# Computing the first memory attention's keys and values at the start of the kernel instead of under the recurrence

## The chip, the cores and the metric

The kernel runs on one core of a Trainium2 chip. Its time is device microseconds for one execution; three runs gave 3854.62, 3855.39 and 3858.6 us, and the median, 3855.39 us, is the time before. A core has five engines with a queue each: TensorE (PE, matrix products), VectorE (DVE), ScalarE (ACT), GpSimd (POOL) and SyncE (SP, which here issues most transfers). Sixteen DMA engines carry all transfers between DRAM and on-chip memory.

## The reference

Two stacks run one after the other on 256 tokens of width 2048, in float32. The first is two layers of attention with pooling and Fourier branches; each layer is modulated by a shift, a scale and a gate that come from a condition vector. The second has an even layer (sparse attention and an RWKV recurrence, joined by one output projection), an odd layer (a state space mixer), and after each a cross attention to 256 memory tokens and an MLP. The two pieces that the change touches are the memory's keys and values and the projection:

```python
shift, scale, gate = jnp.split(jax.nn.silu(c) @ ada_w[l] + ada_b[l], 3, axis=-1)   # first stack
h = rmsnorm(x, norm_g[l]) * (1.0 + scale[:, None]) + shift[:, None]

mix = jnp.concatenate([y_a, y_b], axis=-1) @ even_w_out[i]                         # second stack, even layer
x = x + mix
kv = (rms_norm(mem, norm_mem[layer]) @ wkv).reshape(bsz, mem.shape[1], 2, X_HEADS, X_HEAD_DIM)
```

The memory does not depend on anything that the kernel computes, so its keys and values can be had at any time. `y_a @ even_w_out[:1024]`, half of the output projection, is ready to run once the sparse attention is done; the recurrence gives `y_b`.

## The kernel before, in words

Every large product follows one pattern. `raw` (L309 to L315) issues one transfer of 512 KB of weights from SP into a tile `wraw`; `split` (L303) has ACT cast it into a high part `wh` (L308) and DVE subtract that to a low part `wl` (L309); PE multiplies high by high, high by low and low by high into PSUM tiles `acc` (L344 to L352, or L392 and L393 in `dense_p`). In the first stack there are three buffers of each of `wraw`, `wh` and `wl`; PSUM has four `acc` and four `sm`.

At the start (`layer1`, L780 on, with `l = 0`) the kernel loads the residual `xc` by eight transfers on ACT's queue, squares it for its norm, and streams 64 tiles of the condition's weights `ada_w`, 512 KB each, through three kinds of buffer in turn (`STAGS`: `wraw`, `wl`, `ada_raw`); each feeds two short matmuls (L543). From the twentieth tile in program order on, a step of the first product with `w_in` (`pool_gen`) follows every eighth tile. The tokens are modulated in four groups (`scaled`), as soon as their columns of the condition are there.

A queue of background generators `bg` fills in elsewhere: `tick` advances its first entry, at a lower priority. The instructions of all engines are then put in order by a scheduler that weighs priorities and estimated times, so that their order is not the one in which the code is written.

In the even layer (`even`, L1487) the recurrence goes: preparation of head group 0 (`rwkv_prep`, `rwkv_mats`), with the second group's keys and values (`rkv_stream`) behind it; preparation of group 1; the inverse of 64x64 triangular blocks (`rwkv_inv`), which is 31 pairs of DVE operations on a tile that went through DRAM (`MD`), with its result back through DRAM (`XD`, `YD`); the scan over chunks (`rwkv_seq`); the finish (`rwkv_fin`). The background under the preparation of group 1 is the half output projection (`dense_p(WO, 0, 8, ...)`, sixteen steps of sixteen matmuls, each pair of steps ending in four adds to the residual, L526). Under the inverse and the scan it is `memkv(0, ...)` (L1596), sixteen steps: eight times, 256 KB of `memT` scaled and split (L489, L490) and multiplied by two tiles of `xattn_wkv`. Its norm's statistic is `mem_stat` (L963), a background of the first layer's end that reads `memT` a first time through `wraw`. The keys and values are written to `kv` after the finish (`mkv[0]()`).

Of the kernel before, what the change touches and what calls it, by code (L numbers as in the profile page):

```python
# [10 lines left out]
F32 = mybir.dt.float32  # L11
# [202 lines left out]
class Prog:  # L214
# [575 lines left out]
    def layer1(self, l, xc, adac, st, st_out):  # L790
# [8 lines left out]
        with ExitStack() as es:  # L799
# [10 lines left out]
            with self.pool(f"pl{l}") as pp, self.pool(f"nrm{l}") as p:  # L810
# [16 lines left out]
                if not last:  # L827
# [7 lines left out]
                    adas = [self.ada(0, part, cb, adac, p) for cb in range(4) for part in range(2)]  # L835
                    for i in range(8 * 8):
                        b, j = divmod(i, 8)
                        next(adas[b])
                        if b and j == SJ:
                            next(adas[b - 1], None)  # L840
                            if b % 2 == 0:
                                scaled(b // 2 - 1)
# [9 lines left out]
                    self.bg.append(self.mem_stat())  # L852
# [110 lines left out]
    def mem_stat(self):  # L963
# [4 lines left out]
        for k in range(0, KT, 2):  # L968
            w = self.wp.tile([128, KB, 512], F32, name="wraw", bufs=self.wraw)[:, :, :T]
            nc.sync.dma_start(w, mT[:, k:k + 2])  # L970
            self.stat_add(st, w)
            yield
# [3 lines left out]
        nc.scalar.copy(self.mrb, self.bcast(self.mrc, 2)[:, :T])  # L976
        yield
# [507 lines left out]
    def even(self, xc, st, kv, st_out):  # L1485
# [4 lines left out]
        with ExitStack() as es:  # L1490
# [32 lines left out]
            with self.pool("rw0") as rp:  # L1523
# [11 lines left out]
                self.bg.append(self.dense_p(WO, 0, 8, 0, D, Xa, self.add_evac(x)))  # L1535
                with self.pool("rw1") as rp1:
# [5 lines left out]
                    with self.pool("rwb") as p:  # L1542
                        mkv = []
                        self.rwkv_room(s1, p)
                        self.rwkv_mats(s1, BKt)
                        self.flush()
                        room = yp.tile([128, 8, 2, T], F32R, name="mem0", tag="ya")
                        self.bg.append(self.memkv(0, kv[0], kv[1], p, room, mkv))
# [12 lines left out]
                        mkv[0]()  # L1561
# [34 lines left out]
    def memkv(self, l, kT, vN, p, room=None, end=None):  # L1596
# [5 lines left out]
        for k0 in range(0, KT, KB):  # L1602
            m = p.tile([128, KB, T], F32, name="mm", bufs=2)
            i = KB * (k0 // KB % 2)
            hl = p.tile([128, KB, 2, T], F32R, name="mhl", bufs=2) if room is None else room[:, i:i + KB]
# [16 lines left out]
        def evac():  # L1622
            for i in range(2):
                nc.vector.tensor_tensor(kT[:, 2 * i:2 * i + 2], ka[i], self.mrb.unsqueeze(1).to_broadcast([128, 2, T]), op=ALU.mult)
                nc.scalar.mul(vN[:, i], va[i], self.mrc[:, i:i + 1])
        if end is None:
            evac()
        else:
            end.append(evac)
# [408 lines left out]
    def body(self):  # L2038
# [13 lines left out]
        self.wraw, self.wbuf = WR, WB  # L2052
        with self.pool("w1") as self.wp, self.pool("b1") as p:
            st = self.first(xc, p)
# [121 lines left out]
```

## Time and profile before

| what | before |
|---|---|
| median of three runs | 3855.39 us |
| profiled execution | 3850.04 us |
| its span | 3848.3 us |
| PE busy / DVE busy / ACT busy | 95% / 70% / 44% of the span |
| mean granted clock of PE | 0.975 of full |
| DMA, whole span | 182 GB/s, 700.74 MB |

The profiled execution's time is 1.7 us more than its span, and all times of the trace are counted from the span's start. A view "by stretch" gives, for each stretch, the time that each engine was busy, then the granted clock of PE, the busy share of the DMA engines and the rate. A view "by line" groups instructions by code line and says what the engine waited for before them. PE's matmuls overlap each other in the trace, so the mean duration of one is longer than the time it adds.

### The profile page before, as it was taken

What the parts mean: (1) busy time and instruction counts of PE and PEld (TensorE: products, weight loads), DVE (VectorE), ACT (ScalarE), POOL (GpSimd) and SP (SyncE); (2) the same over time, 40 slices, a digit from 0 to 9 for tenths busy, and PEclk for the clock granted to TensorE, in tenths of its full rate; (3) what the DMA queues carried; (4) which work ended last, traced back from release to release, by engine and by line L of the source; (5) the groups of instructions that cost most, each with busy time, mean ns of one, the idle gap of its engine ahead of it and who ended that gap; (6) DMA issues with size and microseconds to landing.
All of it is one profiled execution on the core that took longest, in us unless ns stands there. A gap on an engine that the chain in (4) does not pass through costs nothing.

```text
span 3848.3 us, 54892 instructions
## 1 busy us (share of the span) xinstructions
PE 3654.7 (95%) x21008; PEld 3029.0 (79%) x21008; DVE 2694.8 (70%) x4732; ACT 1680.5 (44%) x2524; POOL 102.1 (3%) x138
## 2 busy tenths in 40 slices
PE   6999999989999999899999999999879999999997
PEld 2677777777678889777888888887778788888886
DVE  3568777765776878767987778786666676656565
ACT  3313233262564566425544444444325454445353
POOL 0010000001000001000000000000000000000000
PEclk8999999999999999889999999999989999999999
DMA  9745544555655544524666666668985556666664
GB/s 343 244 145 176 158 149 156 175 170 174 215 152 158 142 137 140 164 67 145 188 214 197 208 200 208 198 211 247 223 197 181 165 154 191 187 191 187 190 186 148
DMA packets 609335, 700.74 MB, mean 182 GB/s; under 512 B 52208, under 2 KB 493680, under 8 KB 605744
## 3 DMA queue, kind: packets, MB, share of 16 engines
q1 hardware_dynamic: 576304, 662.39, 57.1%
q10 hardware_dynamic: 31488, 30.64, 2.4%
q0 software_dynamic: 1280, 4.20, 0.4%
q8 instruction: 165, 2.70, 0.3%
q14 instruction: 98, 0.80, 0.1%
HBM read 672.63 MB, written 24.51 MB: 181 GB/s over the span
## 4 chain that ended last, share of the span: by engine, by line
PE 82%; DMA 9%; DVE 6%; ACT 2%; issue 1%; SPq 0%; ACTq 0%; POOL 0%; DVEq 0%; POOLq 0%
PE acc L392 33%; PE acc L393 17%; PE acc L344 4%; PE acc L345 4%; PE acc L346 4%; PE acc L350 3%; PE acc L352 3%; PE acc L351 3%; DMA wraw<-ada_w 2%; DVE wl L309 2%; PE sm L623 1%; ACT wh L308 1%; PE sm L600 1%; DMA wraw<-w_in 1%; DMA tts<-KD 1%
## 5 line engine op out<-in xcount | busy, mean ns | idle before, releaser
L308 ACT CAST wh<-wraw 128x1024 fp32r<-128x1024 f32 x994 | 1037.7, 1045 | 1486.3 <-PE acc L392 734.1
L309 DVE TENSOR_TENSOR wl<-wraw,wh 128x1024 fp32r<-128x1024 f32 x994 | 1208.5, 1217 | 643.8 <-ACT wh L308 639.6
L392 PE MATMUL acc<-hl,wh 128*128 128x512 f32 x3008 | 1060.4, 400 | 21.9 <-DVE hl L490 15.1
L393 PE MATMUL acc<-hl,wl 128*128 128x256 f32 x3008 | 827.3, 284 | 4.3 <-DVE wl L309 4.3
L392 PE MATMUL acc<-hid,wh 128*128 128x512 f32 x2048 | 709.9, 394 | 1.4 <-DVE xc L526 1.0
L392 PEld LDWEIGHTS acc<-hl,wh 128*128 128x128 f32 x3008 | 559.3, 190 | 150.4 <-DVE hl L490 11.6
L393 PEld LDWEIGHTS acc<-hl,wl 128*128 128x128 f32 x3008 | 567.9, 190 | 23.4 <-DVE wl L309 8.1
L393 PE MATMUL acc<-hid,wl 128*128 128x256 f32 x2048 | 559.8, 280 | 0.0
L392 PEld LDWEIGHTS acc<-hid,wh 128*128 128x128 f32 x2048 | 378.3, 188 | 85.6 <-issue 1.8
L393 PEld LDWEIGHTS acc<-hid,wl 128*128 128x128 f32 x2048 | 380.9, 188 | 9.0 <-issue 3.4
L571 DVE SCALAR_TENSOR_TENSOR ada_a<-wraw,sc,ada_a 128x512 f32<-128x512 f32 x360 | 253.5, 749 | 19.6 <-DMA wraw<-ada_w 18.7
L344 PE MATMUL acc<-hl,wh 128*128 128x512 f32 (+2 forms) x688 | 256.0, 376 | 7.7 <-ACT wh L308 3.8
L345 PE MATMUL acc<-hl,wh 128*128 128x512 f32 (+2 forms) x688 | 252.9, 369 | 0.0
L346 PE MATMUL acc<-hl,wl 128*128 128x512 f32 (+2 forms) x688 | 247.1, 369 | 0.0
L350 PE MATMUL acc<-wh,hl 128*128 128x512 f32 (+1 forms) x504 | 200.1, 402 | 4.0 <-ACT wh L308 2.5
L351 PE MATMUL acc<-wh,hl 128*128 128x512 f32 (+1 forms) x504 | 199.7, 396 | 0.0
L352 PE MATMUL acc<-wl,hl 128*128 128x512 f32 (+1 forms) x504 | 189.2, 395 | 4.4 <-DVE wl L309 4.4
L526 DVE TENSOR_TENSOR xc<-acc,xc 128x256 f32<-128x256 f32 x384 | 141.8, 419 | 36.7 <-PE acc L393 36.1
L344 PEld LDWEIGHTS acc<-hl,wh 128*128 128x128 f32 (+1 forms) x688 | 130.2, 190 | 37.3 <-issue 6.6
L345 PEld LDWEIGHTS acc<-hl,wh 128*128 128x128 f32 (+1 forms) x688 | 130.0, 189 | 25.2 <-issue 5.9
L346 PEld LDWEIGHTS acc<-hl,wl 128*128 128x128 f32 (+1 forms) x688 | 129.1, 189 | 23.9 <-issue 3.2
L406 ACT COPY joined<-acc 128x256 f32<-128x256 f32 x188 | 69.5, 371 | 133.1 <-PE acc L393 133.0
(588 smaller groups left out, 4950.0 us busy)
## 6 DMA issues: line engine op xcount, KB each, us to landing
wraw<-ffn_up SPq DMA_DIRECT2D x256, 512.0 KB, 3.8
wraw<-ffn_down SPq DMA_DIRECT2D x256, 512.0 KB, 3.7
wraw<-ada_w SPq DMA_DIRECT2D x192, 512.0 KB, 4.5
wraw<-w_in SPq DMA_DIRECT2D x144, 512.0 KB, 4.4
wraw<-w_out SPq DMA_DIRECT2D x64, 512.0 KB, 4.5
wraw<-even_w_in SPq DMA_DIRECT2D x54, 512.0 KB, 3.7
wraw<-even_w_out SPq DMA_DIRECT2D x32, 512.0 KB, 3.6
wraw<-xattn_wkv SPq DMA_DIRECT2D x32, 512.0 KB, 4.7
```

The costliest lines, as they stand in the source:

```text
L308: nc.scalar.copy(hi, src)
L309: self.held(nc.vector.tensor_tensor(lo, src, hi.bitcast(F32), op=ALU.subtract))
L344: nc.tensor.matmul(A, h, xh, start=(start and first), stop=False)
L345: nc.tensor.matmul(A, h, xl, start=False, stop=False)
L346: nc.tensor.matmul(A, lo, xh, start=False, stop=(stop and last))
L350: nc.tensor.matmul(A, xh, wh[:, kk, :cw], start=start, stop=False)
L351: nc.tensor.matmul(A, xl, wh[:, kk, :cw], start=False, stop=False)
L352: nc.tensor.matmul(A, xh, wl[:, kk, :cw], start=False, stop=stop)
L392: nc.tensor.matmul(A, wh[:, kk, cs], xp, start=k == 0, stop=False)
L393: nc.tensor.matmul(A[:, 1], wl[:, kk, cs], xp[:, 0], start=False, stop=k == nk - 1)
L526: nc.vector.tensor_tensor(x[:, j + i], A[:, h], x[:, j + i], op=ALU.add)
L571: nc.vector.scalar_tensor_tensor(a[:, r], w[:, kk], c, a[:, r], op0=ALU.mult, op1=ALU.add)
```

## The change

`memkv_first` takes the place of `mem_stat` and of `memkv(0, ...)`: it reads `memT` once, takes the statistic, scales, splits and multiplies by `xattn_wkv`, and is advanced by one step after four of every five of the first condition tiles, before the first product with `w_in`. The four `acc` hold the sums; the scaled memory lies in a part of `hl` that is not yet in use. The results are scaled by the norm's factor at the end of it and written to two DRAM tiles (`kvd`) from POOL's queue; after the finish of the recurrence they are read back on ACT's queue. The half output projection moves from the preparation of group 1 to the inverse and the scan.

```diff
@@ -833,9 +833,12 @@
                             for r in range(2):
                                 modulate(k, r)
                     adas = [self.ada(0, part, cb, adac, p) for cb in range(4) for part in range(2)]
+                    mg = self.memkv_first(hl[:, 12:])
                     for i in range(8 * 8):
                         b, j = divmod(i, 8)
                         next(adas[b])
+                        if i % 5 < 4:
+                            next(mg, None)
                         if b and j == SJ:
                             next(adas[b - 1], None)
                             if b % 2 == 0:
@@ -849,7 +852,6 @@
                     self.step(pg, 7 - (64 - SI + 7) // 8)
                     self.bg.append(self.ada_slow(0, 2, adac))
                     self.bg.extend(self.ada_slow(1, part, self.adac1) for part in range(2))
-                    self.bg.append(self.mem_stat())
...
-    def mem_stat(self):
+    def memkv_first(self, room):
+
 
         nc = self.nc
         st = self.stat()
         mT = self.a["memT"].rearrange("(k p) t -> p k t", p=128)
-        for k in range(0, KT, 2):
-            w = self.wp.tile([128, KB, 512], F32, name="wraw", bufs=self.wraw)[:, :, :T]
-            nc.sync.dma_start(w, mT[:, k:k + 2])
-            self.stat_add(st, w)
-            yield
+        ka = [self.acc((2, T)) for _ in range(2)]
+        va = [self.acc() for _ in range(2)]
+        for k0 in range(0, KT, KB):
+            m = self.wp.tile([128, KB, 512], F32, name="wraw", bufs=self.wraw)[:, :, :T]
+            nc.sync.dma_start(m, mT[:, k0:k0 + KB])
+            self.stat_add(st, m)
+            hl = room[:, k0 // KB % 4].rearrange("p a (b t) -> p a b t", b=2)
+            for i in range(KB):
+                self.scale_split(hl[:, i], m[:, i], self.col("norm_mem0")[:, k0 + i:k0 + i + 1], None)
+            for c0 in (0, 512):
+                wh, wl = self.weights(self.a["xattn_wkv_2"][0], k0 * 128, KB, c0, 512)
+                for kk in range(KB):
+                    first, last = k0 + kk == 0, k0 + kk == KT - 1
+                    if c0 == 0:
+                        self.mm_t(ka, 2, wh, wl, kk, 512, 128, hl[:, kk, 0], hl[:, kk, 1], first, last)
+                        continue
+                    for tb in range(2):
+                        s = slice(tb * 128, tb * 128 + 128)
+                        self.mm_n(va[tb], wh, wl, kk, 512, hl[:, kk, 0, s], hl[:, kk, 1, s], first, last)
+                if c0 == 0 or k0 + KB < KT:
+                    yield
         ss = self.sm((4,))
         self.stat_cols(st, ss, True)
         self.rstd_cols(ss[:, :2], D, 1e-5, self.mrc)
         nc.scalar.copy(self.mrb, self.bcast(self.mrc, 2)[:, :T])
+        for i in range(2):
+            t = self.sqp.tile([128, 2, T], F32, name="sqt", bufs=2)
+            nc.vector.tensor_tensor(t, ka[i], self.mrb.unsqueeze(1).to_broadcast([128, 2, T]), op=ALU.mult)
+            nc.gpsimd.dma_start(self.kvd[0][:, 2 * i:2 * i + 2], t)
+            t = self.sqp.tile([128, 512], F32, name="sqt", bufs=2)
+            nc.scalar.mul(t, va[i], self.mrc[:, i:i + 1])
+            nc.gpsimd.dma_start(self.kvd[1][:, i], t)
         yield
 
...
@@ -1532,7 +1558,6 @@
                         self.rwkv_prep(s0, BKt, wa, p)
                     self.rwkv_mats(s0, BKt)
                     self.flush()
-                self.bg.append(self.dense_p(WO, 0, 8, 0, D, Xa, self.add_evac(x)))
                 with self.pool("rw1") as rp1:
                     s1 = self.rwkv_state(1, rT[1], kT[1], vT[1], rp1)
                     BKt = bkt(1)
@@ -1540,12 +1565,9 @@
                     with self.pool("rwa1") as p:
                         self.rwkv_prep(s1, BKt, wa, p)
                     with self.pool("rwb") as p:
-                        mkv = []
                         self.rwkv_room(s1, p)
                         self.rwkv_mats(s1, BKt)
-                        self.flush()
-                        room = yp.tile([128, 8, 2, T], F32R, name="mem0", tag="ya")
-                        self.bg.append(self.memkv(0, kv[0], kv[1], p, room, mkv))
+                        self.bg.append(self.dense_p(WO, 0, 8, 0, D, Xa, self.add_evac(x)))
                         self.hold = True
                         _, self.fill_inv, self.fill_seq = FB
                         self.rwkv_inv((s0, s1), bkt(2), p)
@@ -1558,7 +1580,8 @@
                         self.hold = False
                         for s in (s0, s1):
                             self.rwkv_fin(s, g2, gl)
-                        mkv[0]()
+            nc.scalar.dma_start(kv[0], self.kvd[0])
+            nc.scalar.dma_start(kv[1], self.kvd[1])
             yb = yp.tile([128, 8, 2, T], F32R, name="yb", tag="ya")
...
+        kd = pool("kvd", space=DRAM)
+        self.kvd = kd.tile([128, 4, T], F32, name="kd"), kd.tile([128, 2, 512], F32, name="vd")
```

The rest of the diff takes the arguments `room` and `end` out of `memkv`, which the odd layer still uses.

How the order moves, at three places. A count at the end of a row is that of equal instructions in a row. First SP's queue at the start of the program; `ada_w` is the condition's weights, `w_in` those of the first product. Before:

```order
L314 DMA wraw<-ada_w 128x2x512 x22
L314 DMA wraw<-w_in 128x2x512
L314 DMA wraw<-ada_w 128x2x512 x7
L314 DMA wraw<-w_in 128x2x512
L314 DMA wraw<-ada_w 128x2x512 x9
```

Now, from the same place:

```order
L314 DMA wraw<-ada_w 128x2x512
L975 DMA wraw<-memT 128x2x256
L314 DMA wraw<-xattn_wkv 128x2x512
L314 DMA wraw<-ada_w 128x2x512 x2
L314 DMA wraw<-xattn_wkv 128x2x512
L314 DMA wraw<-ada_w 128x2x512
L975 DMA wraw<-memT 128x2x256
L314 DMA wraw<-xattn_wkv 128x2x512
L314 DMA wraw<-ada_w 128x2x512 x2
L314 DMA wraw<-xattn_wkv 128x2x512
L975 DMA wraw<-memT 128x2x256
L314 DMA wraw<-xattn_wkv 128x2x512
```

The sixteen tiles of `xattn_wkv` and the eight of `memT` stand ahead of the first `w_in`, among 21 condition tiles (22 before); from the first `w_in` on the order of the two kinds is as it was, but for a few exchanges of neighbours.

Second ACT's queue at the start, from the last six of the residual's eight transfers on; `L448` squares, `sqt` and `sqacc` are its results. Before:

```order
L2072 DMA xc<-xc 128x4x256 x6
L2075 DMA rows<-rows 128x512
L2076 DMA consts_90<-consts 128x512
L448 ACTIVATE sqacc<-xc 128x512
L448 ACTIVATE sqt<-xc 128x512 x2
L736 DMA poolM<-k_pool 128x2048
```

Now:

```order
L2091 DMA xc<-xc 128x4x256 x6
L2094 DMA rows<-rows 128x512
L2095 DMA consts_94<-consts 128x512
L489 ACTIVATE hl<-wraw,cols 128x256 x2
L308 CAST wh<-wraw 128x1024
L736 DMA poolM<-k_pool 128x2048
L738 DMA poolW<-pool_w 128x4x128
L765 DMA dftn<-k_dftn 128x1024
L767 DMA dftc<-k_dftc 128x256
L448 ACTIVATE sqacc<-xc 128x512
L448 ACTIVATE sqt<-xc 128x512 x2
L448 ACTIVATE sqacc<-wraw 128x512
```

The first scaling of the memory (`hl<-wraw`) and the first cast stand behind the residual's transfers; the square of the first memory tile (`sqacc<-wraw`) stands behind three squares of the residual.

Third PE's queue in the preparation of group 1, from the end of `rkv_stream` on; `ya` is the half output projection, `mhl` the stream, the rest is the preparation (`kbh`, `vT`, `kp`, `lw`, `rne`). Before, a piece of it:

```order
L392 MATMUL acc<-ya,wh 128x512
L393 MATMUL acc<-ya,wl 128x256
L392 MATMUL acc<-ya,wh 128x512 x2
L1312 MATMUL sm<-consts,vT_9073 128x128 x2
L1319 MATMUL sm<-kp,consts_9064 128x256
L1266 MATMUL sm<-consts_9064,lw 128x256 x2
L393 MATMUL acc<-ya,wl 128x256 x2
L392 MATMUL acc<-ya,wh 128x512
L393 MATMUL acc<-ya,wl 128x256
L392 MATMUL acc<-ya,wh 128x512
L393 MATMUL acc<-ya,wl 128x256
L392 MATMUL acc<-ya,wh 128x512
```

Now:

```order
L346 MATMUL acc<-mhl,wl 128x256
L392 MATMUL acc<-ya,wh 128x512 x2
L1338 MATMUL sm<-consts,vT_9509 128x128 x2
L1345 MATMUL sm<-kp,consts_9500 128x256
L1292 MATMUL sm<-consts_9500,lw 128x256 x2
L1307 MATMUL sm<-consts,rne 128x128 x2
L1330 MATMUL sm<-consts,kbh 128x128 x2
L1338 MATMUL sm<-consts,vT_9509 128x128 x2
L1345 MATMUL sm<-kp,consts_9500 128x256
L1292 MATMUL sm<-consts_9500,lw 128x256 x2
L1330 MATMUL sm<-consts,kbh 128x128 x4
L1307 MATMUL sm<-consts,rne 128x128 x2
```

The projection's matmuls that stood between the preparation's are gone but for the first two; the next 128 of them stand behind the last product of `rwkv_mats`.

## Rows read from the trace of the kernel before

**Rows 1.** The page: span, PE, granted clock and DMA share in forty slices (tenths).

```profile
span 3848.3 us, 54892 instructions
...
PE 3654.7 (95%) x21008; PEld 3029.0 (79%) x21008; DVE 2694.8 (70%) x4732; ACT 1680.5 (44%) x2524; POOL 102.1 (3%) x138
...
PE   6999999989999999899999999999879999999997
...
PEclk8999999999999999889999999999989999999999
DMA  9745544555655544524666666668985556666664
...
PE 82%; DMA 9%; DVE 6%; ACT 2%; issue 1%; SPq 0%; ACTq 0%; POOL 0%; DVEq 0%; POOLq 0%
```

**Rows 2.** Busy time by stretch at the front; stretch in us, then its length.

```profile
core 0: us, PE busy (x) PEld busy (x) DVE busy (x) ACT busy (x) POOL busy (x), PEclk, DMA share, GB/s
0.00:5.00 5.00, 0.00 (x0) 0.00 (x0) 0.48 (x1) 0.00 (x0) 0.20 (x4) 1.00 0.60 180
5.00:45.60 40.60, 18.18 (x64) 3.23 (x64) 10.63 (x18) 11.71 (x20) 0.00 (x0) 0.79 1.06 374
45.60:62.00 16.40, 13.18 (x61) 6.29 (x62) 7.46 (x22) 8.05 (x18) 1.01 (x1) 0.90 1.05 386
62.00:100.00 38.00, 33.52 (x165) 17.39 (x164) 11.44 (x35) 11.86 (x25) 0.00 (x0) 0.96 0.87 300
```

**Rows 3.** PE by line, first 46 us; busy, mean ns, idle before and releasers.

```profile
L543 PE MATMUL sm<-wraw,sc 128*32 128x512 f32 x62 | 17.8, 801 | 14.3 <-DMA wraw<-ada_w 7.4 <-ACT sc L2066 6.9
```

**Rows 4.** Timeline of the front; start us, us, engine, line, operation, idle before.

```profile
7.03 17.42 ACTq L2072 DMA_DIRECT2D xc<-xc  x5
...
30.24 0.63 ACT L448 ACTIVATE sqacc<-xc 128x512 f32<-128x512 f32 x1 [23.36 <-DMA xc<-xc]
...
45.61 0.42 SPq L314 DMA_DIRECT2D wraw<-w_in  x1
...
58.47 1.22 PE L350 MATMUL acc<-wh,hl 128*128 128x512 f32 x2
```

**Rows 5.** Busy time by stretch, recurrence and the memory statistic; columns as rows 2.

```profile
1524.50:1564.60 40.10, 39.95 (x247) 34.54 (x246) 37.99 (x87) 25.68 (x60) 4.48 (x9) 1.00 0.47 146
1564.60:1579.30 14.70, 14.70 (x170) 12.70 (x169) 10.72 (x25) 3.46 (x4) 1.12 (x2) 1.00 0.66 188
1579.30:1615.40 36.10, 28.25 (x142) 22.29 (x140) 34.37 (x85) 12.52 (x18) 0.00 (x0) 0.86 0.47 140
...
1636.30:1699.00 62.70, 62.70 (x724) 56.67 (x724) 39.57 (x67) 15.58 (x22) 3.28 (x2) 0.98 0.25 82
...
750.00:780.00 30.00, 26.61 (x116) 21.40 (x115) 15.92 (x23) 11.25 (x15) 2.90 (x4) 1.00 0.57 180
```

**Rows 6.** DMA issues, whole span; count, KB each, median us to landing.

```profile
wraw<-xattn_wkv SPq DMA_DIRECT2D x32, 512.0 KB, 4.7
...
wraw<-memT SPq DMA_DIRECT2D x8, 256.0 KB, 4.1
```

**Rows 7.** DVE by line, 1524.5 to 1564.6 us; columns as rows 3.

```profile
L309 DVE TENSOR_TENSOR wl<-wraw,wh 128x1024 fp32r<-128x1024 f32 x12 | 14.6, 1217 | 1.0 <-ACT wh L308 1.0
L526 DVE TENSOR_TENSOR xc<-acc,xc 128x256 f32<-128x256 f32 x20 | 7.8, 416 | 0.2 <-PE acc L393 0.2
```

**Rows 8.** ACT by line, 1524.5 to 1564.6 us.

```profile
L308 ACT CAST wh<-wraw 128x1024 fp32r<-128x1024 f32 x11 | 11.6, 1056 | 9.9 <-PE acc L392 6.8 <-PE acc L345 1.8 <-ACT wh L308 0.6
```

**Rows 9.** Timeline of ACT, two casts while the projection alone fills.

```profile
1570.59 1.05 ACT L308 CAST wh<-wraw 128x1024 fp32r<-128x1024 f32 x1 [6.62 <-PE acc L392]
1573.39 1.05 ACT L308 CAST wh<-wraw 128x1024 fp32r<-128x1024 f32 x1 [1.75 <-PE acc L392]
```

**Rows 10.** DVE by line, the inverse, 1579.3 to 1615.4 us.

```profile
L309 DVE TENSOR_TENSOR wl<-wraw,wh 128x1024 fp32r<-128x1024 f32 x7 | 8.5, 1218 | 0.0
L490 DVE SCALAR_TENSOR_TENSOR mem<-mm,cols,mem 128x256 fp32r<-128x256 f32 x7 | 3.2, 478 | 0.0
L526 DVE TENSOR_TENSOR xc<-acc,xc 128x256 f32<-128x256 f32 x8 | 3.2, 417 | 0.0
```

More of the change, by code (lines that the diff above doesn't have):

```diff
@@ L1593, in middle_norm, with memkv @@
                 yield
-    def memkv(self, l, kT, vN, p, room=None, end=None):
+    def memkv(self, l, kT, vN, p):
         nc = self.nc
@@ L1603, in memkv @@
             m = p.tile([128, KB, T], F32, name="mm", bufs=2)
-            i = KB * (k0 // KB % 2)
-            hl = p.tile([128, KB, 2, T], F32R, name="mhl", bufs=2) if room is None else room[:, i:i + KB]
+            hl = p.tile([128, KB, 2, T], F32R, name="mhl", bufs=2)
             nc.sync.dma_start(m, self.a["memT"].rearrange("(k p) t -> p k t", p=128)[:, k0:k0 + KB])
@@ L1620, in memkv @@
                     yield
[L1622 to L1629, printed above, removed]
+        for i in range(2):
+            nc.vector.tensor_tensor(kT[:, 2 * i:2 * i + 2], ka[i], self.mrb.unsqueeze(1).to_broadcast([128, 2, T]), op=ALU.mult)
+            nc.scalar.mul(vN[:, i], va[i], self.mrc[:, i:i + 1])
         yield
```

## The prediction

> **What bounds the kernel now.** I read the page first: TensorE (PE) is busy for 95% of a span of 3848.3 us, and only the first of the forty slices has it at 6 tenths; in that slice the DMA engines are at 9 tenths and PE's granted clock is below full [rows 1]. So nearly everywhere a change pays by taking matmuls or PE's gaps away, and the front is a place of its own. Then I cut the front into stretches. From 5 to 45.6 us the DMA share is 1.06 at 374 GB/s while PE is busy 18.18 us of 40.6; from 45.6 to 62 us it is still 1.05; from 62 to 100 us the rate is 300 GB/s and PE is busy 33.52 of 38 us [rows 2]. The front therefore waits for bytes. What PE does there says the same: its 62 condition records up to 46 us have 7.4 us of idling for tiles of `ada_w` ahead of them, and the 6.9 us beside it is one wait for the condition itself at the start [rows 3]. The order of events in the front: ACT issues the residual's eight transfers, its first square runs at 30.24 us, the first tile of `w_in` is issued at 45.61 us, and its first matmul runs at 58.47 us [rows 4].
>
> The second place is the recurrence at about 1525 to 1700 us. There I cut by what DVE does, because PE is busy through all of it but the middle: preparation of the second head group (1524.5 to 1564.6), products and the round trip through DRAM (1564.6 to 1579.3), the inverse (1579.3 to 1615.4), the scan (1636.3 to 1699) [rows 5].
>
> **What the change adds: the front.** Sixteen tiles of `xattn_wkv` of 512 KB and eight of `memT` of 256 KB [rows 6] go ahead of the first tile of `w_in` on SP's queue. That is 16 x 0.524 + 8 x 0.262 = 10.5 MB. Up to 45.6 us the kernel moved 5 x 0.18 + 40.6 x 0.374 = 16.1 MB [rows 2]; now 26.6 MB must pass before the same tile.
>
> Lower end: at the saturated 374 GB/s, 10.5 MB are 28 us. Nothing makes it less as long as SP's order holds, since the copies of `memT` that the later statistic read are not in this stretch.
>
> Upper end: the memory's tiles use only the three `wraw` buffers. One use lasts a landing (4.7 us for `xattn_wkv` [rows 6]), a subtraction on DVE (1.22) and a cast on ACT (1.06) [rows 7, 8], about 7 us. With a third of the 21 condition tiles of the stretch there are 24 + 7 = 31 uses. The first `memT` tile is released only after ACT has read it, and on ACT that stands behind the eight residual transfers and, for its square, behind three squares of the residual, so at about 30 us [rows 4]. SP's second `memT` needs that buffer, and everything on SP behind it waits: the remaining 28 uses take 28 x 7 / 3 = 65 us, so the first `w_in` tile goes out at 95 us, a delay of 50 us.
>
> Value: the rate of 62 to 100 us, a stretch that also mixes tiles which wait for engines, is 300 GB/s; 26.6 MB at that rate are 89 us, a delay of 43 us. I take it because it is the measured stretch most like the new one and lies between the ends.
>
> PE does not set this: a step of an output projection is one cast period, 1573.39 - 1570.59 = 2.8 us [rows 9]; a memory step has the same columns (24 x 256 or 12 x 512 against 8 x 512 + 8 x 256), so sixteen are 45 us, and beside them 21 condition tiles of four records at 17.8 / 62 = 0.29 us [rows 3], 24 us: 69 us, less than the 89. What follows the first `w_in` tile keeps its order, with the gains of the first quarter now computed beside the last memory steps, so I carry the delay through to the end. The results go out in four transfers on POOL's queue, which has next to nothing else, and come back on ACT behind the scan; I cost both at nothing, covered by the second half of the output projection, and one wait of a landing, about 5 us, if not.
>
> *A rule against the change.* The row shows SP's and ACT's transfers together at 374 GB/s with a share of 1.06 [rows 2]. The Trainium skill, "DMA: Bandwidth & Descriptors", section "Rules for kernel authors", holds that transfers issued from several engines run on the same 16 DMA engines, so that a second queue brings no bandwidth; the trace agrees. The same page, section "Measured (HBM→SBUF, 128 partitions, SWDGE, issued from GpSimd)", gives 425 GB/s for one core with large transfers: by that the lower end would be an estimated 25 us instead of 28, and the sum would be 3 us less at that end. The rows never show more than 386, so the sum goes by them.
>
> **What it moves and removes: the recurrence.** The half output projection leaves the preparation and replaces the memory work under inverse and scan. The order has only two of its matmuls left in the preparation.
>
> Preparation: 40.1 us, DVE busy 37.99 [rows 5]. The twelve weight subtractions (14.6 us) and twenty adds (7.8 us) go [rows 7], which leaves DVE 15.6 us; ACT keeps 25.68 - 11.6 = 14.1 us [rows 5, 8]. So the stretch ends between 15.6 us (no waits left) and 40.1 us (its chain DVE, ACT, PE, ACT over four column groups was the bound all along). I take 26, close to the middle, since with two groups in flight DVE must now wait for ACT's exponentials: a gain of 14, ends 0 and 24.5. What is late next is that chain.
>
> Products and round trip: 14.7 us; less traffic beside the DRAM trip, but an idle PE may have lost its clock. No change taken, 2 us either way.
>
> Inverse: DVE is busy 34.37 of 36.1 us, so this is DVE's [rows 5]. The seven scaled ones for `mem` (3.2 us) go, and of seven subtractions that go with a cast six stay in the new order (1.2 us); eight adds before, eight after [rows 10]. Gain 4.4, ends 0 and 4.4. All sixteen steps of the filler have the same PE time as before, and about half of them fall behind the inverse in both orders, so the scan, where PE is busy throughout [rows 5], stays.
>
> Statistic of the memory: it leaves 750 to 780 us, where its tiles shared `wraw` with `w_out` and PE idled 30 - 26.6 = 3.4 us [rows 5]. I take 3.4, ends 0 and 5.
>
> Sum: +43 - 14 - 4.4 - 3.4 = +21 us. The profiled execution took 3850.04 us (span 3848.3 and 1.7 around it), so it would be 3871; the median of the runs, 3855.39, lies 5.35 above that execution, so the forecast is 3877 us.
>
> **Rivals.**
> *Faster: PE was the front's bound after all.* Then the 45 us of memory work fill gaps. Up to 62 us PE idles 5 + 22.4 + 3.2 = 30.6 us [rows 2]; with all of that used, the front is 14 us later, and with the preparation at its floor the recurrence and the statistic give 24.5 + 4.4 + 3.4 = 32. Time 3855 - 18 = 3837. It decides as soon as the front's delay is under the rear's gain. For it: the gaps are real, and PE's clock was 0.79 there. Against it: a DMA share of 1.05 to 1.06 up to 62 us leaves no room for 10.5 MB.
>
> *No change.* The lower end of the front, 28 us, against a rear between its middle and its floor, 22 to 32: 3851 to 3861. For it: SP keeps many tiles in flight in the kernel before. Against it: memory tiles hold `wraw` much longer than a condition tile does.
>
> *Worse: the buffers set the front.* A delay of 50 us and a rear that gives only 5 to 10, as its own chain of four groups was the bound: +40 to +45, 3895 to 3900. For it: SP issues in order, so that one held tile stops the condition too; against it, ACT may pass the residual's transfers sooner when SP is stopped and the bandwidth is theirs.
>
> *The change doesn't do what it says:* the scheduler could put the projection back into the preparation. The order excludes it but for two matmuls.
>
> **How the numbers follow.** Forecast 0.60, from 3863 to 3893. Faster rival 0.13; no change 0.14; worse 0.13. A difference under 0.2% (7.7 us) can't be told from none here. Faster 0.13, the same 0.14, slower 0.60 + 0.13 = 0.73. All bounds together are 28 - 34 = -6 to 50 - 0 = +50, that is 3849 to 3905; the range is 3848 to 3903, which leaves out the faster rival and the outer edge of the worse one.
>
> **What would show it.** In the new profile: the first tile of `w_in` issued at about 89 us (74: the lower end; 95 or later: the buffers); a DMA share in 5 to 45 us below 1 if buffers hold SP, at 1.05 if bytes do; the distance from the last matmul of the key/value stream to the first `M` on DVE at 26 us instead of 40; the inverse at 32 us; no PE gap of the kind at 750 to 780 us. The forecast is wrong if `w_in` starts before 70 us or if the recurrence gives back more than 30 us.

## The result, and the profile of the changed kernel

The changed kernel takes 3881.21 us (median of five runs, 3876.0 to 3893.81); the ratio to the kernel before is 1.0078, 95% interval 1.0065 to 1.009, so it is 25 to 35 us slower. The two medians alone give 1.0067; that of the kernel before is of five runs here and still 3855.39 us. The forecast was 3877 in a range of 3848 to 3903. Its profiled execution took 3888.01 us, that of the kernel before 3850.04, so the two traces differ by 37.9 us in span, more than the medians do. That matters below, where terms are read from the traces.

The page of the changed kernel, the lines that answer to [rows 1]:

```profile
span 3886.2 us, 54885 instructions
...
PE 3666.6 (94%) x21008; PEld 3043.0 (78%) x21008; DVE 2696.3 (69%) x4732; ACT 1679.4 (43%) x2524; POOL 105.8 (3%) x142
...
PE   6899999999899999699999999999879999999997
...
PEclk9999999999999999889999999999989999999999
DMA  8955454645655454234566766668995546666664
...
PE 82%; DMA 8%; DVE 6%; ACT 2%; issue 1%; SPq 1%; ACTq 0%; POOL 0%; DVEq 0%; POOLq 0%
```
PE's busy time grew by 12 us and the span by 38, so 26 us more are idle. PE's first slice is as it was, its second fell from 9 tenths to 8; the 17th, the recurrence, fell from 8 tenths to 6. DMA at the front is busy for longer, not harder.

The front by stretches, columns as in [rows 2]:

```profile
core 0: us, PE busy (x) PEld busy (x) DVE busy (x) ACT busy (x) POOL busy (x), PEclk, DMA share, GB/s
0.00:5.00 5.00, 0.00 (x0) 0.00 (x0) 0.48 (x1) 0.00 (x0) 0.20 (x4) 1.00 0.59 175
5.00:45.60 40.60, 19.01 (x79) 13.25 (x80) 17.59 (x25) 19.20 (x32) 0.00 (x0) 0.94 0.97 329
45.60:62.00 16.40, 13.27 (x66) 7.96 (x65) 6.16 (x9) 5.06 (x7) 0.00 (x0) 0.92 0.76 249
62.00:100.00 38.00, 35.31 (x202) 25.92 (x199) 15.73 (x30) 14.79 (x22) 1.01 (x1) 0.92 0.79 264
...
140.00:200.00 60.00, 53.82 (x267) 29.30 (x260) 28.47 (x68) 26.79 (x53) 0.00 (x0) 0.97 0.95 335
```
From 5 to 45.6 us the rate is 329 GB/s, and then it falls to 249 and 264. PE idles 5 + 21.6 + 3.1 + 2.7 = 32 us up to 100 us, where the kernel before idled 31 us up to 62 us [rows 2]: the memory's matmuls did not go into the gaps, they took the place of the condition's, of which 16 run from 5 to 45.6 us where 60 did before. From 140 to 200 us the DMA share is still 0.95 (0.51 in the kernel before).

What SP waited for most from 45.6 to 101 us (total, times, longest):

```profile
SPq L314 <- PE sm L543: 15.5, 7, 4.2
SPq L314 <- DVE wl L309: 7.3, 5, 2.4
SPq L975 <- DVE wl L309: 6.5, 4, 2.4
SPq L314 <- DVE hl L490: 5.4, 6, 1.0
```
These 35 of 55 us went to buffers whose tile PE or DVE was still reading, while the DMA share was 0.76 to 0.79. Before its first `w_in` tile the kernel before waited 1.3 us in that way, and DMA was at 1.06.

The events of the front, from two stretches of the timeline (start, length, engine, line):

```profile
6.61 9.20 ACTq L2091 DMA_DIRECT2D xc<-xc  x5
...
18.71 0.51 ACT L489 ACTIVATE hl<-wraw,cols 128x256 fp32r<-128x256 f32 x1 [12.06 <-DMA xc<-xc]
...
19.52 1.03 ACT L308 CAST wh<-wraw 128x1024 fp32r<-128x1024 f32 x1
...
101.09 0.37 SPq L314 DMA_DIRECT2D wraw<-w_in  x1
...
108.82 0.39 PE L352 MATMUL acc<-wl,hl 128*128 128x512 f32 x1
...
110.39 1.49 POOL L465 TENSOR_TENSOR mrc<-mrc,consts 128x2 f32<-128x2 f32 x1 [14.49 <-DVE mrc L1007]
...
112.95 0.69 ACT L1001 ACTIVATE sqt<-acc,mrc 128x512 f32<-128x512 f32 x1
113.08 0.69 DVE L998 TENSOR_TENSOR sqt<-acc,mrb 128x512 f32<-128x512 f32 x1 [1.30 <-ACT mrb L995]
...
115.13 0.50 PE L350 MATMUL acc<-wh,hl 128*128 128x512 f32 x1
```
ACT issued residual transfers until 15.8 us and made its first cast for the memory at 19.5. The first tile of `w_in` went out at 101.09 us instead of 45.61 [rows 4]. It landed at 104.9 and its first matmul ran at 115.13, just after L998 and L1001 had scaled the results out of the first two of the four accumulators (the other two followed at 123.3 and 124.6); in the kernel before the matmul was at 58.47. The last memory matmul ended at 109.2: some 4 us between it and the scaling went to the norm's factor, 1.5 of them on POOL.

The second place, in the order of [rows 5]: preparation, products and round trip, inverse, scan, and last the stretch that answers to 750 to 780 us.

```profile
1574.50:1603.80 29.30, 16.91 (x81) 12.96 (x81) 19.35 (x55) 14.21 (x47) 4.62 (x9) 0.77 0.02 6
1603.80:1617.70 13.90, 5.74 (x112) 5.36 (x112) 5.78 (x17) 1.44 (x4) 1.11 (x2) 0.75 0.24 58
1617.70:1650.80 33.10, 20.23 (x90) 16.52 (x91) 31.11 (x78) 5.24 (x5) 0.00 (x0) 0.79 0.30 92
1671.80:1735.00 63.20, 63.20 (x691) 55.71 (x687) 41.26 (x74) 13.73 (x18) 4.13 (x2) 0.97 0.27 85
804.10:834.10 30.00, 30.00 (x134) 24.81 (x134) 13.33 (x19) 8.63 (x10) 2.89 (x4) 1.00 0.56 181
```
The preparation takes 29.3 us instead of 40.1, with PE busy for 16.91 of them and its clock at 0.77; products 13.9 (14.7); inverse 33.1 (36.1); scan 63.2 (62.7). Where the memory's statistic had been, PE now has no gap.

The start of the same transfer in two traces, this one less that of the kernel before, shows where time is lost and won along the whole kernel (us; the other columns are experiments below):

| transfer (its start before) | changed | e1 | e2 | e3 | e14 | e12 |
|---|---|---|---|---|---|---|
| first `w_in` tile (45.6) | +55.5 | -0.2 | +47.7 | +19.0 | +53.8 | +33.6 |
| 65th `w_in` tile (528) | +54.2 | -2.3 | +39.7 | +31.1 | +49.3 | +29.9 |
| 81st `w_in` tile (834) | +49.5 | -7.5 | +35.9 | +25.3 | +43.6 | +25.3 |
| 65th `even_w_in` tile (1492) | +46.9 | -0.7 | +37.2 | +25.3 | +43.6 | +25.6 |
| first `xattn_wq` tile (1760) | +33.7 | -14.4 | +19.1 | +15.8 | +8.3 | +4.9 |
| 241st `ffn_down` tile (3770) | +37.6 | -11.4 | +23.0 | +15.2 | +6.1 | -0.3 |

### The profile page after: what moved, and what is told of

It reads as the page before. It is cut to its first block, busy times and chain, and to the rows that moved or that the text cites. A ratio compares the mean times of both kernels' runs of the same rounds, so it can differ in the third digit from the quotient of the medians.

```text
span 3886.2 us, 54885 instructions
## 1 busy us (share of the span) xinstructions
PE 3666.6 (94%) x21008; PEld 3043.0 (78%) x21008; DVE 2696.3 (69%) x4732; ACT 1679.4 (43%) x2524; POOL 105.8 (3%) x142
## 4 chain that ended last, share of the span: by engine, by line
PE 82%; DMA 8%; DVE 6%; ACT 2%; issue 1%; SPq 1%; ACTq 0%; POOL 0%; DVEq 0%; POOLq 0%
PE acc L392 33%; PE acc L393 17%; PE acc L344 4%; PE acc L345 4%; PE acc L346 4%; PE acc L350 3%; PE acc L352 3%; PE acc L351 3%; DVE wl L309 2%; DMA wraw<-w_in 2%; DMA wraw<-ada_w 1%; PE sm L623 1%; ACT wh L308 1%; PE sm L600 1%; DMA wraw<-xattn_wkv 1%
## 5 line engine op out<-in xcount | busy, mean ns | idle before, releaser
L392 PEld LDWEIGHTS acc<-hl,wh 128*128 128x128 f32 x3008 | 559.6, 190 | 151.1 <-DVE hl L490 11.6
L393 PEld LDWEIGHTS acc<-hl,wl 128*128 128x128 f32 x3008 | 568.3, 190 | 24.8 <-DVE wl L309 8.8
L344 PE MATMUL acc<-hl,wh 128*128 128x512 f32 (+1 forms) x752 | 274.7, 370 | 19.6 <-ACT wh L308 15.8
L345 PE MATMUL acc<-hl,wh 128*128 128x512 f32 (+1 forms) x752 | 273.0, 365 | 0.0
L571 DVE SCALAR_TENSOR_TENSOR ada_a<-wraw,sc,ada_a 128x512 f32<-128x512 f32 x360 | 254.1, 751 | 23.1 <-DMA wraw<-ada_w 22.6
L346 PE MATMUL acc<-hl,wl 128*128 128x512 f32 (+1 forms) x752 | 266.8, 365 | 0.6 <-DVE wl L309 0.5
L350 PE MATMUL acc<-wh,hl 128*128 128x512 f32 (+1 forms) x536 | 216.0, 407 | 15.3 <-ACT wh L308 13.4
L351 PE MATMUL acc<-wh,hl 128*128 128x512 f32 (+1 forms) x536 | 212.8, 397 | 0.0
L352 PE MATMUL acc<-wl,hl 128*128 128x512 f32 (+1 forms) x536 | 202.6, 398 | 4.2 <-DVE wl L309 4.2
L344 PEld LDWEIGHTS acc<-hl,wh 128*128 128x128 f32 x752 | 144.0, 192 | 51.9 <-ACT wh L308 21.2
L526 DVE TENSOR_TENSOR xc<-acc,xc 128x256 f32<-128x256 f32 x384 | 141.8, 421 | 40.6 <-PE acc L393 40.0
L346 PEld LDWEIGHTS acc<-hl,wl 128*128 128x128 f32 x752 | 142.3, 191 | 29.4 <-issue 7.0
L345 PEld LDWEIGHTS acc<-hl,wh 128*128 128x128 f32 x752 | 143.9, 192 | 25.7 <-issue 6.1
L350 PEld LDWEIGHTS acc<-wh,hl 128*128 128x128 f32 x536 | 103.4, 193 | 49.1 <-ACT wh L308 18.1
```

The costliest lines, as they stand in the source:

```text
L344: nc.tensor.matmul(A, h, xh, start=(start and first), stop=False)
L345: nc.tensor.matmul(A, h, xl, start=False, stop=False)
L346: nc.tensor.matmul(A, lo, xh, start=False, stop=(stop and last))
L350: nc.tensor.matmul(A, xh, wh[:, kk, :cw], start=start, stop=False)
L351: nc.tensor.matmul(A, xl, wh[:, kk, :cw], start=False, stop=False)
L352: nc.tensor.matmul(A, xh, wl[:, kk, :cw], start=False, stop=stop)
```

## The experiments

Times are medians; each ratio is to runs of the kernel before on the same chip. In the cuts of code `...` stands for what is left out, and the comments are added.

| kernel | us | ratio, 95% |
|---|---|---|
| changed | 3881.2 | 1.0078 (1.0065 to 1.0090) |
| e1, no memory work | 3832.1 | 0.9952 (0.9938 to 0.9967) |
| e2, memory's bytes only | 3874.1 | 1.0059 (1.0042 to 1.0076) |
| e3, memory's work without bytes | 3865.6 | 1.0033 (1.0020 to 1.0046) |
| e4, own buffers | 3875.0 | 1.0054 (1.0035 to 1.0074) |
| e9, own buffers, residual on POOL | 3878.3 | 1.0062 (1.0041 to 1.0082) |
| e6, projection in the preparation | 3855.4 | 1.0014 (0.9999 to 1.0028) |
| e14, the same again | 3861.5 | 1.0027 (1.0015 to 1.0038) |
| e13, the same, own buffers | 3866.0 | 1.0038 (1.0025 to 1.0051) |
| e10, projection shared out | 3864.4 | 1.0036 (1.0022 to 1.0051) |
| e11, the same, own buffers | 3867.2 | 1.0039 (1.0026 to 1.0052) |
| e12, keys alone at the front | 3853.4 | 1.0007 (0.9994 to 1.0020) |
| e8, before with the statistic moved | 3863.1 | 1.0020 (1.0008 to 1.0032) |

**e1: the memory's work left out.** `memkv_first` keeps only its stores, of constants:
```
-        for k0 in range(0, KT, KB): ...
+            nc.vector.memset(t, 1.0)
```


> The changed kernel with the memory's keys and values left out of the front (constants are stored instead, so the output is not the reference's). It shows what the rest of the change is worth by itself. My theory: the front's delay comes from the memory work alone and the rear's gain is what the two traces show, some 5 us at 750 to 780 us and 13 us in the recurrence. Then the first w_in tile goes out at about 46 us again and the time is 3855 - 20 = 3835 us (3830 to 3842). Rival: the recurrence's gain depends on the later start, or on noise between the two profiled executions; then 3845 to 3856 us.

3832 us, as expected: the rest of the change is worth 18.5 us (13 to 24), and the front starts as it did (-0.2 us). So the loss is the memory's work at the front and nothing else. By the ratios it costs 1.0078 - 0.9952 = 1.26%, some 48 us.

**e2 and e3: that work split into its bytes and its instructions.** In e2 the 24 transfers stay and nobody reads them; in e3 everything else stays and reads one tile that is loaded once (`one`).
```
e2:                self.raw(self.a["xattn_wkv_2"][0], k0 * 128, KB, c0, 512)
e3: +              self.split(wh, wl, one)
```


> The memory's 24 transfers stay where the change put them, in the same buffers and the same order on SP, but nothing reads them (constants are stored as keys and values). Bytes theory (my prediction's main term): the front is as late as in the changed kernel or nearly, first w_in tile at 85 to 101 us, time 3872 to 3881 us. Buffer and order theory: without readers a buffer is free at its landing, the delay falls to the bytes at the full rate, 28 us or less; first w_in tile at 74 us or before, time 3850 to 3863 us.

> The opposite half: all casts, subtractions, squares and matmuls of the memory stay, but they read one tile that is loaded once, so 23 of the 24 transfers are gone (the output is not the reference's). Bytes theory: the front's delay nearly goes, at most the 15 us by which 45 us of matmuls exceed the 30 us of gaps; 3835 to 3850 us. Theory of matmuls that can't enter the gaps (the four accumulators are held by the memory until its last step, and ACT's casts stand behind the residual's transfers): first w_in matmul 30 to 45 us later than before, time 3862 to 3881 us.

Against e1, on the same chip, the bytes alone cost 1.07%, 41 us, and the instructions alone 0.81%, 31 us; together 48, so that they run beside each other for 24, and the bytes are the longer, though by little (the intervals of e2 and e3 touch). The buffer theory had e2 at 3863 or less and fell; the bytes theory in its pure form had e3 at 3850 or less and fell too. e3 came out as the theory of held accumulators had it. The front of e2 by stretches, one row of what SP waited for up to 93 us (total, times, longest), and three events:

```profile
5.00:45.60 40.60, 9.25 (x24) 1.14 (x24) 11.35 (x17) 11.37 (x19) 0.98 (x2) 1.00 1.01 346
45.60:62.00 16.40, 2.08 (x10) 0.20 (x8) 0.00 (x0) 0.59 (x1) 1.39 (x3) 1.00 1.00 357
62.00:98.20 36.20, 20.49 (x78) 7.14 (x80) 2.67 (x13) 1.20 (x3) 1.04 (x1) 0.68 0.85 292
```
```profile
SPq L314 <- DMA wraw<-xattn_wkv: 16.5, 6, 4.2
```
```profile
93.26 0.37 SPq L314 DMA_DIRECT2D wraw<-w_in  x1
...
98.18 1.04 ACT L308 CAST wh<-wraw 128x1024 fp32r<-128x1024 f32 x1 [2.70 <-DMA wraw<-w_in]
...
101.06 0.74 PE L350 MATMUL acc<-wh,hl 128*128 128x512 f32 x2 [0.19 <-ACT hl L308]
```
The DMA engines are nearly as busy up to 62 us as in the kernel before (1.01 and 1.00), with PE busy for 9 us of 40: this is bytes. After that the rate is 292 GB/s; over the whole front SP waits 16.5 us for an unread `xattn_wkv` tile to land before the next one may use its buffer. So the three buffers still count without readers; no run gave the memory's tiles more than three. From landing (98.2) to the matmul (101.1) it takes 3 us, as in the kernel before; the 10 us of the changed kernel belong to its accumulators. e3's front by stretches, and its first `w_in` matmul:

```profile
5.00:45.60 40.60, 22.68 (x120) 17.59 (x121) 22.07 (x34) 24.59 (x43) 0.00 (x0) 1.00 0.83 288
45.60:62.00 16.40, 16.40 (x110) 11.72 (x112) 11.42 (x19) 9.93 (x15) 0.00 (x0) 1.00 0.66 216
62.00:85.00 23.00, 23.00 (x148) 15.98 (x141) 8.49 (x13) 4.90 (x6) 1.01 (x1) 1.00 0.56 190
```
```profile
92.85 0.50 PE L350 MATMUL acc<-wh,hl 128*128 128x512 f32 x1
```
Here the DMA engines have room (0.83, 0.66, 0.56), and PE is busy without a gap from 45.6 to 85 us. The memory's matmuls begin at 22.8 us, since ACT, in line with the residual, makes its first cast at 21.7, and `w_in` cannot start before they end, as `ka` and `va` hold all four `acc` buffers: its first tile landed at 70.2 and waited 22.6 us for its matmul, 34 us later than in the kernel before.

**e4 and e9: buffers, and ACT's place in line.** e4 gives the memory's tiles three raw buffers of their own; e9 also issues the residual's transfers on POOL.
```
e4: -      m = self.wp.tile(..., name="wraw", bufs=self.wraw)
e4: +      m = raw[n % 3][:, :, :T]
e9: -      nc.scalar.dma_start(xc[:, r, 4 * q:4 * q + 4], ...)
e9: +      nc.gpsimd.dma_start(xc[:, r, 4 * q:4 * q + 4], ...)
```


> The changed kernel, but the memory's tiles land in three raw buffers of their own instead of the three that the condition and w_in share; all on SP's queue as before. Buffer theory (what held SP in the front was that a condition or w_in tile waits for a buffer that a memory tile holds): first w_in matmul 10 to 25 us sooner than in the changed kernel, time 3857 to 3871 us. Rival, SP's own order is the hold, since a memory tile that waits for its own buffer stops the queue as well, or ACT, which casts nothing before 19 us: within 5 us of the changed kernel, 3876 to 3884 us.

> As the kernel with own buffers, and the residual's eight transfers are issued by POOL instead of ACT. In the changed kernel ACT issued them one by one until 15.9 us and made its first memory cast at 19.5 us. Theory that ACT's place in line costs the first 10 us: the first cast at 8 to 10 us, and the time 6 to 12 us under that of own buffers alone. Rival, bytes: the memory's tiles and the residual share one rate, so what comes sooner of the one makes the other late; within 4 us of own buffers alone.

e4's 3875 us lies in neither expected range; its interval overlaps the changed kernel's, and own buffers won nothing in e13 against e14 or in e11 against e10: they are worth nothing that shows. e4's first `w_in` tile goes out 27 us sooner, but that is another order: seven memory tiles stand behind it, and the last of them goes out at 94.5 us (96.2 in the changed kernel). Its matmul comes 6 us sooner (SP, then PE):

```profile
74.18 1.66 SPq L314 DMA_DIRECT2D wraw<-w_in  x1
...
94.47 0.37 SPq L986 DMA_DIRECT2D third<-xattn_wkv  x1
```
```profile
109.11 0.50 PE L350 MATMUL acc<-wh,hl 128*128 128x512 f32 x1
```
The tile waits for the accumulators, which the tiles behind it still fill. Whether readers that hold buffers set the front is not decided by e4, for its memory tiles wait for their own three buffers on the same queue. In e9 ACT's first cast came at 14.0 us, not at the 8 to 10 expected, and the time did not improve (1.0062 against 1.0054), as the rival had it: from 5 to 45.6 us e9 moved 354 GB/s, e4 362. The Trainium skill, "DMA: Bandwidth & Descriptors", "Rules for kernel authors", says that spreading transfers over the queues of SP, ACT and GpSimd brings no bandwidth; e9's rate agrees.

**e6 and e14: the front of the change alone.** One program, run twice: the projection is put back where it was, and nothing fills inverse and scan.
```
+                self.bg.append(self.dense_p(WO, 0, 8, ...))   # ahead of the preparation
-                        self.bg.append(self.dense_p(WO, 0, 8, ...))   # ahead of the inverse
+                        self.flush()
```


> The front of the change alone: the half output projection goes back into the preparation of the second head group, and nothing fills the inverse and the scan. Theory that TensorE's work bounds the recurrence: the preparation is 10 us longer again (29 to 40 us), the scan loses eight filler steps of 2.8 us and ends up to 22 us sooner; time 3865 to 3881 us, about 3870. Rival, chains of DVE bound inverse and scan anyway: the preparation's 10 us come on top, 3887 to 3895 us.

> The kernel with the projection in the preparation once more, beside the two others on one chip: its profiled execution took 3874.68 us where the nine others had a median of 3855. Expected 3852 to 3860 us again; the profiled execution, if it is near that, shows where the 18 us were, else the spread stays unexplained.

20 to 26 us faster than the changed kernel, more than the 10 that were expected; the rival fell. e14's 3861.5 us is just above the 3852 to 3860 expected. e14's preparation, inverse and scan, and e6's scan:

```profile
1568.00:1608.30 40.30, 39.85 (x247) 34.66 (x246) 38.16 (x88) 25.62 (x60) 4.48 (x9) 1.00 0.47 147
1623.00:1652.80 29.80, 5.60 (x31) 4.36 (x30) 27.78 (x74) 2.82 (x3) 0.00 (x0) 0.63 0.27 84
1667.70:1709.00 41.30, 39.39 (x589) 37.80 (x588) 25.82 (x51) 6.04 (x11) 3.24 (x2) 0.95 0.05 15
...
1678.10:1722.80 44.70, 42.77 (x592) 41.05 (x587) 25.79 (x50) 6.04 (x11) 3.24 (x2) 0.87 0.04 14
```
The preparation is back at 40 us with PE busy for 39.85 of them; the scan, without filler, takes 41.3 us instead of 63. So the scan was PE's, its eight filler steps cost 22 us, and the change had left that much lying there: it moved the projection from a stretch where sixteen steps cost 11 us to one where half of them cost 22. The profiled executions of e6 and e14, one program, differ by 18 us: 5 at the front, 1 at the statistic, 9 in the recurrence, 2 to 3 later. Of the 9, 3.4 are the scan, which ran at a granted clock of 0.87 in e6 and 0.95 in e14. What makes such a spread stayed open; terms under some 10 us cannot be taken from one pair of traces.

**e10, e11, e13: the projection shared out, own buffers.**
```
e10: +                  self.step(wo, 8)      # eight steps beside the preparation
e10: +                  self.bg.append(wo)    # the other eight under the inverse
```


> The changed kernel with the half output projection shared out: eight of its sixteen steps beside the preparation of the second head group, eight under the inverse, none in the scan. Theory (each stretch has room for so many steps at no cost: about 21 us of idle TensorE in the changed kernel's preparation and round trip, 32 us in the empty inverse of the kernel with the projection all in the preparation, none in the scan): the scan stays at 37 us, the preparation falls back to some 30 us, the inverse grows by 3 to 4 us; 20 to 30 us under the changed kernel and 5 to 10 under the one with all of it in the preparation, 3845 to 3852 us. Rival: filler under the inverse delays DVE's chain there as much as it spares elsewhere; 3853 to 3862 us.

> The same, and the memory's tiles of the front in three raw buffers of their own. If the two edits add, it is 6 us under the shared projection alone, 3838 to 3847 us, faster than both kernels. Rival: the front is bound by bytes and its accumulators, and the 6 us of the own buffers were the spread of single executions; then it is within 3 us of the shared projection alone.

> The projection in the preparation, and the memory's tiles of the front in three raw buffers of their own. Own buffers brought 6 us in one pair of kernels and none in the other. If they are worth something at the front, this is 4 to 8 us under the same kernel without them, 3846 to 3852 us; if bytes and accumulators set the front, within 3 us of it.

e10 is no better than e14 and missed its 3845 to 3852 by 12 us (it lies above its rival's range too); own buffers brought nothing on top, in e11 or in e13. e10's preparation, inverse and scan:

```profile
1567.50:1604.60 37.10, 34.71 (x221) 29.86 (x221) 32.34 (x80) 23.59 (x58) 4.47 (x9) 0.97 0.38 116
1617.40:1653.00 35.60, 22.48 (x91) 18.63 (x92) 30.81 (x77) 5.24 (x5) 0.00 (x0) 0.73 0.27 85
1671.50:1716.70 45.20, 42.53 (x580) 40.71 (x579) 25.57 (x50) 5.68 (x10) 3.24 (x2) 0.86 0.07 21
```
The preparation gains only 3 us on e14's, the inverse pays 6, and the scan, with the same instructions, takes 4 us more at a clock of 0.86 against 0.95. e6's scan, which is e14's program, was as long at the same clock, so the 4 us are no cost of sharing out; its preparation and inverse (40.3 and 30.0 us) are e14's, so the 3 and the 6 stand. By the medians the room that I had counted as free was not.

**e12: half the memory at the front.** The keys stay there; the values, eight steps, go under the inverse, and the projection into the preparation.
```
-            for c0 in (0, 512):
+            wh, wl = self.weights(self.a["xattn_wkv_2"][0], k0 * 128, KB, 0, 512)
+                        self.bg.append(self.memv(kv[1], p, room, mkv))   # ahead of the inverse
```


> The keys alone are computed at the front (6.3 MB instead of 10.5, eight steps instead of sixteen, two accumulators instead of four); the values, eight steps, fill the inverse; the half output projection is back in the preparation and nothing fills the scan. If the front is bound by bytes first, it gives back 4.2 MB at some 250 GB/s, 17 us, and the filler under the inverse costs the 6 to 10 us that eight steps cost there in the shared kernel: 3842 to 3852 us, under the kernel with all of the memory at the front and the projection in the preparation, and perhaps under the kernel before. Rival: the front's delay is a chain that does not shrink with its bytes, or the inverse pays for its filler what the front saves; 3853 to 3862 us.

The first `w_in` tile goes out at 79.16 us, and the front costs 30 us in place of 49 to 54 (table of starts): 4.2 MB, eight steps and two held accumulators less are worth 19 us or more; which of the three gives how much is not separated. Inverse and scan of e12:

```profile
79.16 0.37 SPq L314 DMA_DIRECT2D wraw<-w_in  x1
```
```profile
1607.60:1645.60 38.00, 27.62 (x100) 19.14 (x98) 36.28 (x90) 14.29 (x23) 0.00 (x0) 0.87 0.47 148
1664.20:1705.70 41.50, 38.87 (x566) 37.36 (x566) 25.56 (x50) 5.69 (x10) 3.24 (x2) 0.95 0.09 27
```
The scan stays at 41.5 us, and the inverse takes 38.0 (29.8 in e14): the front saved what was expected and the inverse took 8 of it back. The whole is 1.0007 (0.9994 to 1.0020), at the lower edge of the rival's 3853 to 3862 us: the lowest of the arrangements with memory at the front, though e6's interval overlaps, and no different from the kernel before. None of the runs that compute the memory beats the kernel before.

**e8: the statistic alone.** The kernel before, without `mem_stat`; `memkv(0)` squares the tiles that it loads anyway.
```
+            if l == 0:
+                self.stat_add(sm, m)
```


> The kernel before, with one part alone: the memory's statistic is taken from the memory tiles that its own keys and values load anyway under inverse and scan, so the 2 MB of transfers, squares and adds at 750 to 780 us go. Theory: the 5 us that the changed kernel gained there come, and the squares and adds hide in the scan, where DVE was busy 39.6 of 62.7 us; 3850 us (3846 to 3853), faster than both kernels. Rival: the squares and adds lengthen the inverse, where DVE is busy nearly throughout, by 8 x (0.7 + waits), and take the gain back; 3853 to 3859 us.

The rival held, and more: 1.0020. The inverse, 36.1 us before, and the squares' adds in it:

```profile
1582.50:1626.00 43.50, 27.89 (x144) 22.79 (x142) 38.58 (x91) 14.63 (x22) 0.00 (x0) 0.83 0.40 130
```
```profile
L453 DVE TENSOR_TENSOR sqacc<-sqacc,sqt 128x512 f32<-128x512 f32 x4 | 2.8, 693 | 2.8 <-ACT sqt L448 2.8
```
The gap at 750 us was won, but the inverse paid 7 us, 2.8 of them for four adds and 2.8 for the squares that these wait for. What follows the scan was 10 us longer as well (41.1 us from the last product with the gate on DVE to the first `xattn_wq` tile, 30.7 before); the statistic is finished there now, ahead of the scaling, but no run separates that.

## Why the prediction was right, and where it was not

**The front, forecast +43, measured +48 by ratios, +54 in the pair of traces.** The main term was right: more bytes ahead of `w_in` in a queue that keeps its order cost 41 us by themselves (e2). But the work on them was nearer than "PE does not set this" had it: without the bytes it costs 31 (e3). In the traces the first `w_in` matmul is 56.7 us later, 14 more than forecast, from three steps. First, "now 26.6 MB must pass before the same tile" counts bytes up to the issue of the tile. What counts is its landing, at 55.07 us in the kernel before: by then 0.9 + 15.2 + 9.5 x 0.386 = 19.7 MB had passed [rows 2], 3.6 MB more than I counted, since they were on their way. With them 30.2 MB at 300 GB/s give 101 us, a delay of 46: 3 of the 14. Second, the rate: the tile landed at 104.9, at a mean of 282 GB/s (5 x 0.175 + 40.6 x 0.329 + 16.4 x 0.249 + 42.9 x 0.264 = 29.6 MB), 4 more. The rest, 7 us, is the wait at the accumulators, which the working left out with "what follows the first `w_in` tile keeps its order". The lower end, 28 us at the full rate, is not reached even by unread tiles (41).

**The rival "the buffers set the front"** gave 95 us for the first `w_in` tile; it went out at 101. Both signs that the prediction named for it came, a tile at 95 us or later and a DMA share below 1 from 5 to 45 us (0.97), and SP's waits show that from 45.6 us on readers held the buffers. So it is not refuted. Against it as the only cause stands e2: with no reader at all the delay falls only from 48 to 41 us. How bytes and buffers share these 41 us stays open, since no run gave the memory's tiles more than three. The rival's time was too high because it let the rear give only 5 to 10 us, where e1 has 18.5.

**The preparation, forecast 26 us, measured 29.3:** a gain of 10.8 in place of 14. In this execution 3 us of it were lost just ahead: from the 63rd `even_w_in` tile to the first `M` it takes 72.6 us, 80.2 before, but 69.7 and 69.4 in e1 and e4, which run the same code there. DVE is busy for 19 of the 29 us, so the chain is what is left, as forecast. **Products:** 0.8 gained, none forecast. **Inverse:** 3.0 in place of 4.4. **Scan:** unchanged, as forecast. **Statistic:** 4.7 between the 65th and the 81st `w_in` tile, 3.4 forecast. **Reload:** from the scan's end on nothing is lost (the shift of 33.7 us at `xattn_wq` is 33.9 at the first feed-forward tile).

**The sum.** In the traces: +54.2 - 4.7 - 2.6 (834 to 1492 us) - 13.2 + 3.9 (the later layer) = +37.6. The -2.6 and the +3.9 differ in size and sign from kernel to kernel (table) and were not traced to a cause. By medians the change is +26, by the ratio +30; the forecast was +21 on the trace, carried over to the medians. The front's error of 5 and the rest's of 3 (21.8 forecast, 18.5 in e1) have the same sign and add up to 8; that the time came within 4 us of the forecast is partly luck, the spread of executions.

**What the prediction did not see:** it costed the scan as unchanged, which was right, and so did not ask what the scan would have been without filler. From the 65th `even_w_in` tile to the first `xattn_wq` tile the changed kernel is 13 us shorter than before, e14 35 us.

## What to carry to other kernels

Work put ahead of a stream delayed it here by its bytes over the rate of the new stretch (282 GB/s, not the 374 of the old one), counted from landing to landing, and by the accumulators that it held; PE's 31 us of gaps absorbed none of it. Before filler is moved from one stretch to another, ask of each which engine sets it with and without filler: here sixteen steps cost 11 us beside the preparation, eight cost 22 in the scan and 6 to 8 under the inverse.

## What the hardware showed that was not expected

Where PE lost its filler, its granted clock fell with it: 1.00 to 0.77 in the preparation, 1.00 to 0.75 in products and round trip, 0.86 to 0.63 in the empty inverse of e14 (means over both levels, 1.2 and 2.4 GHz), in stretches in which it idled for 42%, 59% and 81% of the time. The prediction had allowed 2 us for it in the products alone. And one program ran the same scan at 0.87 in 44.7 us (e6) and at 0.95 in 41.3 us (e14); why the clock differed is not shown.
